# A 64-byte shift for weight units read in 256 columns, and a weight ring taken in strict turn

## The chip, the cores and the metric

The kernel runs on one core of one Trainium2 chip. The metric is the time of one execution in microseconds (us) on the device. Before the change it is 1171.04 us, the median of three runs (1170.99 to 1173.9).

## What is computed

A two-layer transformer block stack over 256 latent tokens and 256 context tokens of width 1024, batch 1, all in fp32. Layer 0 mixes with retention (4 heads, queries and keys of 256, values of 512), layer 1 with neighbourhood attention (32 heads of 32) over a window of the 4 x 64 grid and all context tokens. Each layer ends with an MLP of hidden width 4096 with a squared ReLU. Cut to what matters here:

```python
p = h_lat @ w_in                                # neighbourhood attention, layer 1
q = p[..., :d].reshape(b, rows, GRID_W, nh, hd) * scale
k = p[..., d:2 * d].reshape(b, rows, GRID_W, nh, hd)
v = p[..., 2 * d:].reshape(b, rows, GRID_W, nh, hd)
pc = h_ctx @ (w_in if ctx_out else w_in[:, d:]) # the context gives keys and values too
...
h = jnp.square(jax.nn.relu(x @ w1)) @ w2        # MLP, sketched: 1024 to 4096 to 1024
```

## The kernel before

**Products in three passes.** Every fp32 operand is split into a rounded part `hi` and a remainder `lo`, and `mm3` forms a product as hi·hi + hi·lo + lo·hi, three matmuls into the same PSUM bank. The activations stand transposed in `hTh` and `hTl` (feature by token, 8 chunks of 512 tokens: 256 latent, then 256 context). A product over latent tokens or context tokens alone is 256 columns wide, one over both is 512.

**Weights in units.** `specs` lists the weights in the order in which they are used, as units of 1024 floats per partition (512 KB in all). `fetch(n)` issues the next n: SP's DMA brings the unit into one of four `raw` buffers, ACT copies it to `hi` (a CAST to the matmul's type), and `lows(n)` later lets DVE subtract `hi` from `raw` into `lo`. The tiles come from the pools `hip` and `lop` of WB = 5 buffers each: a new unit gets the buffer that comes free first. The first stage (`class Weights`, layer 0's first head) takes from the same pools. ACT's CAST has to wait until PE has read the buffer's earlier unit for the last time.

**Order.** In the long retention stage a scheduler places instructions; from the end of layer 0's MLP on, `ORDER = (pe, act, dve)` keeps PE, ACT and DVE in the order in which the code is written, so that an instruction that waits holds up all behind it on its engine. SP and POOL have an order of their own.

**Stages by time.** Retention fills the span to about 440 us, layer 0's MLP runs to 792 us, attention to 990 us and layer 1's MLP to the end. The MLP's first half works on 256 hidden features at a time (a pair of 128): `mm1` on latent tokens and on context tokens apart for the first two pairs, on all 512 columns for the others.

**The start of attention.** The units there are, in order: query pair 0 (2 units), first key group pair (2), query pair 1 (2), first values (4), and so on. `q_mm(p, u)` multiplies query pair p by its unit u for the latent tokens, `q_evac(p)` moves the result to `qT` (four ACT instructions for the high part, eight on DVE for the low part). `k_mm(g, a, b)` multiplies the keys of group g by tokens a to b, `k_evac` moves them to `kT`, and `k_part` does both; the context part of the first keys is late. `scores(0)` then multiplies `kT` by `qT` (bank `pqk`) in three passes of four small matmuls: hi·hi, q-hi·k-lo, q-lo·k-hi, and `v_part` multiplies the values (bank `pnv`). The code runs:

```python
    q_mm(1, 0)
    fetch(2)
    lows(1)
    q_mm(1, 1)
    q_evac(1)
    lows(1)
    ...
    for g in range(2):
        fetch(1)
        k_part(g, NLAT, NT)
        lows(1)
```

followed by `scores(0)`, `fetch(1)`, `soften(0)` and `v_part(0, 0)`. The four fetches in this piece are the four units of the first values; the two query units were taken before.

**A shift that is there already.** In layer 1's MLP the first product reads `hTh` from `AT = 7 * LINE` floats into each chunk on (`LINE` is 16 floats, 64 bytes), so that its 256 columns start 448 bytes into a chunk. Elsewhere a 256-column matmul's moving columns and its stationary weights start at the same remainder of 128 bytes.

**Small constants.** `lnT`, `cT`, `scol`, `bcol`, `acol`, `misc`, `lgn` and four `mods` are single tiles in `cpool`, which lies ahead of the big tiles in SBUF.

Of the kernel before, what the change touches and what calls it, by code (L numbers as in the profile page):

```python
# [10 lines left out]
F32 = mybir.dt.float32  # L11
F32R = mybir.dt.float32r
# [5 lines left out]
P = 128  # L18
D = 1024
KC = D // P  # L20
# [4 lines left out]
DK = 256  # L25
DV = 512
# [10 lines left out]
LINE = 16  # L37
# [67 lines left out]
def kernel(  # L105
# [27 lines left out]
    ec = ctx.enter_context  # L133

    WB = 5
    smp = ec(tc.tile_pool(name="smp", bufs=4))
    cpool = ec(tc.tile_pool(name="cpool", bufs=1))
    rawp = ec(tc.tile_pool(name="rawp", bufs=4))
    hip = ec(tc.tile_pool(name="hip", bufs=WB))
    lop = ec(tc.tile_pool(name="lop", bufs=WB))  # L140
    scp = ec(tc.tile_pool(name="scp", bufs=8))
    arena = ec(tc.tile_pool(name="arena", bufs=1))
    dram = ec(tc.tile_pool(name="dram", bufs=1, space=DRAM))
# [8 lines left out]
    def nm(s):  # L152
        uid[0] += 1
        return f"{s}_{uid[0]}"
# [4 lines left out]
    def slot(i, shape, dt, s):  # L159

        return arena.tile(shape, dt, tag=f"s{i}", name=nm(s))

    def scr(s, dt=F32):
        return scp.tile([P, 512], dt, tag="scr", name=nm(s))
# [17 lines left out]

    specs = []

    def w_rows(wt, r0, nr, c0, ncol):
        specs.append((wt[r0 : r0 + nr, c0 : c0 + ncol], nr // P, ncol))

    WI, WO = ret_w_in[0], ret_w_o[0]
    for h in range(RH):
        if h:  # L190
            for u in range(2):
                w_rows(WI, 512 * u, 512, h * DK, DK)
        for u in range(2):
            w_rows(WI, 512 * u, 512, D + h * DK, DK)
        if h:
            for u in range(4):
                w_rows(WI, 256 * u, 256, 2 * D + h * DV, DV)
        for u in range(4):
            w_rows(WI, 256 * u, 256, 4 * D + h * DV, DV)
        for half in range(2):  # L200
            for u in range(2):
                w_rows(WO, h * DV + u * 256, 256, half * 512, 512)

    def spec_w1(l, f0):
        for u in range(2):
            w_rows(mlp_w1[l], 512 * u, 512, f0, 256)

    for hf in range(2):
        for fp in range(8):
            spec_w1(0, hf * 2048 + fp * 256)  # L210
        for half in range(2):
            for u in range(8):
                w_rows(mlp_w2[0], hf * 2048 + u * 256, 256, half * 512, 512)

    NW, NWO = nat_w_in[0], nat_w_o[0]

    def spec_nq(base, gp):
        for u in range(2):
            w_rows(NW, 512 * u, 512, base + gp * 256, 256)

    def spec_nv(half):
        for u in range(4):
# [2 lines left out]
    for kind, i in (  # L225
        ("q", 0), ("k", 0), ("q", 1), ("v", 0), ("k", 1), ("k", 2), ("q", 2), ("v", 1), ("q", 3), ("k", 3)
    ):
        if kind == "v":
            spec_nv(i)
        else:  # L230
            spec_nq(D if kind == "k" else 0, i)
# [4 lines left out]
    for fp in range(16):  # L236
        spec_w1(1, fp * 256)
# [16 lines left out]
    units = []  # L254
# [3 lines left out]
    def fetch(n, in_scratch=False, at=None):  # L258

        for src, k, ncol in specs[len(units) : len(units) + max(n, 0)]:  # L260
            raw = rawp.tile([P, k, ncol], F32, tag="raw", name=nm("raw"))
            sp.dma_start(out=raw[:], in_=src.rearrange("(k p) n -> p k n", p=P))
            if len(units) in scaled_units:
                dve.tensor_mul(
                    out=raw[:], in0=raw[:], in1=scale_row[0].unsqueeze(1).broadcast_to([P, k, ncol])
                )
            if in_scratch or len(units) in scratch_units:
                hi, lo = Rows([scr("hi", F32R) for _ in range(k)]), Rows([scr("lo", F32R) for _ in range(k)])
                for i in range(k):
                    act.copy(out=hi[:, i, :], in_=raw[:, i, :])  # L270
                    pending.append((lo[:, i, :], raw[:, i, :], hi[:, i, :]))
                units.append((hi, lo))
                continue
            if at is None:
                hi = hip.tile([P, k, ncol], F32R, tag="hi", name=nm("hi"))
                lo = lop.tile([P, k, ncol], F32R, tag="lo", name=nm("lo"))
            else:
                both = slot(at, [P, 2, k, ncol], F32R, "hilo")
                hi, lo = both[:, 0], both[:, 1]
            act.copy(out=hi[:], in_=raw[:])  # L280
            pending.append((lo[:], raw[:], hi[:]))
            units.append((hi, lo))
# [32 lines left out]

    ident = cv("ident")

    lnT = cpool.tile([P, 2, 2, 2, KC], F32, tag="lnT", name="lnT")
    cT = cpool.tile([P, KC, 16, 2], F32, tag="cT", name="cT")
    scol = cpool.tile([P, 2, KC], F32, tag="scol", name="scol")  # L320
    bcol = cpool.tile([P, 2, KC], F32, tag="bcol", name="bcol")
    acol = cpool.tile([P, 3, 2, KC], F32, tag="acol", name="acol")
    COLUMNS = (0, 1), (1, 0), (1, 1)
    lns = dram.tile([64, P], F32, tag="lns", name="lns")

# [40 lines left out]
    still = scr("still", F32R)  # L366
    dve.memset(still[:, :256].bitcast(F32), 1.0)

    misc = cpool.tile([P, 40], F32, tag="misc", name="misc")
    mhalf, onecol, lgm = misc[:, 0:1], misc[:, 1:34], misc[:, 36:40]  # L370
    dve.memset(mhalf[:], -0.5)

    lgn = cpool.tile([P, 2, 8], F32, tag="lgn", name="lgn")
    mods = {}
    for l in range(2):
        for w in range(2):
            mods[l, w] = cpool.tile([P, 2, KC, 2], F32, tag=f"mod{l}{w}", name=f"mod{l}{w}")

# [13 lines left out]
    def outside():  # L394
        rows = rpb_in.rearrange("h d c -> h (d c)")
        parts = [slot(i, [P, 4 * NT], F32, "rows") for i in (S_TH, S_TL)]
        neg = parts[0][:, 4 * NT - 2 * P :]
        for r in range(4):
# [121 lines left out]
    def bg_stream():  # L520
# [13 lines left out]
        for step, (l, w, part, offs, n) in enumerate(plan):  # L534
# [7 lines left out]
            if (l, w, part) in EARLY:  # L542
                dve.on = True
                for kk in range(2):
                    for t in range(nt):
                        weigh(spare(t), raw[:, kk, :], t, 2 * (n % 4) + kk, n % 4 == 0 and kk == 0)
                dve.on = False
                if n % 4 == 3:
                    yield
                    for t in range(nt):  # L550
                        folded(red, spare(t), t, 512 * (n // 4), 512)
            else:
                if n == 0:
                    acc = slot(S_VL, [P, 2, D], F32, "acc")
                for t in range(nt):

                    dve.on = n == 0 and (w, part) == (0, 0)
                    weigh(acc[:, t], raw[:].rearrange("p a n -> p (a n)"), t, n, n == 0)
                    dve.on = False
                if n == KC - 1:  # L560
                    for t in range(nt):
                        folded(red, acc[:, t], t, 0, D)
# [118 lines left out]
    def moments(t):  # L681
        mv = smp.tile([P, 2], F32, tag="mv", name=nm("mv"))
        dve.bn_aggr(out=mv[:], in_=stats[t][:])
        return mv, rstd_of(mv, dve)
# [67 lines left out]
    class Weights:  # L752
# [9 lines left out]

        def high(self, cols=slice(0, DK + DV)):
            if cols.start == 0:
                self.hi = hip.tile([P, DK + DV], F32R, tag="hi", name=nm("hi"))
            act.copy(out=self.hi[:, cols], in_=self.raw[:, cols])

        def low(self, cols=slice(0, DK + DV)):
            if cols.start == 0:
                self.lo = lop.tile([P, DK + DV], F32R, tag="lo", name=nm("lo"))  # L770
            dve.tensor_sub(out=self.lo[:, cols], in0=self.raw[:, cols], in1=self.hi[:, cols].bitcast(F32))

    def chunk_loads(k):
# [147 lines left out]
    w = ws[0]  # L921
# [98 lines left out]
    for h in range(RH):  # L1020
# [9 lines left out]
        else:  # L1030
# [15 lines left out]
            for u in range(4):  # L1046
                ((wh, wl),) = take(1)
                for t in range(4):
                    for kk in range(2):
                        k = 2 * u + kk  # L1050
# [137 lines left out]
        else:  # L1188
# [17 lines left out]
            def turn(t):  # L1206
                return [mod_pt(xns[t], half) for half in range(2)]

            def affine(t, pts):
                return [mod_aff(pts[half], half, t, A, B) for half in range(2)]  # L1210
# [19 lines left out]
            f0 = affine(0, p0)  # L1230
# [11 lines left out]
            for half in range(2):  # L1242
                mod_split(f1[half], half, 1, dve)
            take(0, 2)
            fetch(1)
            white(2, shift_of(*m2), m2[1])
            add_to(3, 0, proj(3, 0), pool)
# [5 lines left out]
    def squared(ps, sl):  # L1253
        w = sl.stop - sl.start
        r = scr("r")
        act.activation(out=r[:, :w], in_=ps[:, sl], func=AF.Relu)
        dve.scalar_tensor_tensor(
            out=r[:, :w], in0=ps[:, sl], scalar=0.0, in1=r[:, :w], op0=ALU.max, op1=ALU.mult
        )
        return r[:, :w]  # L1260
# [31 lines left out]
    for hf in range(2):  # L1292
# [9 lines left out]
        if hf == 0:  # L1302
# [18 lines left out]
            r0 = [squared(pb, LAT) for pb in pbs[0]]  # L1321
# [37 lines left out]
        for half in range(2):  # L1359
# [66 lines left out]
            p = turn(0)  # L1426
            mm2(2, 5, held[1])
            f = affine(0, p)
# [7 lines left out]
            p = turn(1)  # L1436
            f = affine(1, p)
# [422 lines left out]
    n = NS - 1  # L1860
# [74 lines left out]
    mv0, r0 = moments(0)  # L1935
# [300 lines left out]
```

## Time and profile before

| | |
|---|---|
| median of three runs | 1171.04 us (1170.99 to 1173.9) |
| the profiled execution | 1175.97 us |
| its span, first to last instruction | 1174.0 us, so 1.97 us lie outside |
| PE busy | 99% of the span, 6687 matmuls |
| DVE, ACT, POOL busy | 72%, 41%, 16% |
| mean granted TensorE clock | 0.995 of full speed |

The span is that of one execution under the profiler. A stretch of PE's time can be shortened only by fewer or quicker matmuls, or by ending a wait of PE. A group's mean duration of one matmul counts it from issue to the end of its drain; how fast they follow one another is read from the chain, where a piece of n matmuls has one duration.

### The profile page before, as it was taken

To read this page: it belongs to the slowest core of one execution; us is meant where nothing else is said; L and a number is where in the kernel's file an instruction comes from. 1 tells how busy PE (TensorE), PEld (TensorE's weight loads), DVE (VectorE), ACT (ScalarE), POOL (GpSimd) and SP (SyncE) were. 2 spreads that over 40 slices of the span, in tenths; PEclk is the share of its full clock that TensorE was granted. 3 is DMA by queue.
4 is the path that set the end of the run, shared out by engine and by line. 5 is a ranking of instruction groups with operands and counts; after the bars stand their busy time and mean duration, and the time that the engine had idled before them with its cause. 6 is when DMAs were issued, how large, how long until landed. Compare 5 with 4: busy or idle time off the path is not lost.

```text
span 1174.0 us, 17497 instructions
## 1 busy us (share of the span) xinstructions
PE 1163.1 (99%) x6687; PEld 983.5 (84%) x6687; DVE 846.2 (72%) x1393; ACT 476.6 (41%) x833; POOL 193.3 (16%) x352
## 2 busy tenths in 40 slices
PE   9999999999999999999999999999999999999997
PEld 6788888888888889888888888889878878999886
DVE  3796687788798878678866775568566578877456
ACT  2653321332223246442112333137466566756341
POOL 0102001010220237600311011121222221000001
PEclk8999999999999999999999999999999999999999
DMA  9943453545355426636666666625234235666761
GB/s 274 261 146 108 144 172 116 147 140 176 112 174 160 133 72 222 223 114 215 182 213 192 203 211 189 210 90 180 72 116 125 84 111 160 212 207 204 241 198 54
DMA packets 134164, 192.54 MB, mean 164 GB/s; under 512 B 7265, under 2 KB 77489, under 8 KB 134081
## 3 DMA queue, kind: packets, MB, share of 16 engines
q1 hardware_dynamic: 129888, 178.36, 48.5%
q0 software_dynamic: 3136, 10.63, 2.9%
q10 hardware_dynamic: 1056, 2.44, 0.7%
q8 instruction: 52, 0.85, 0.3%
q14 instruction: 32, 0.25, 0.1%
HBM read 185.06 MB, written 6.35 MB: 163 GB/s over the span
## 4 chain that ended last, share of the span: by engine, by line
PE 94%; DVE 2%; ACT 1%; DMA 1%; issue 1%; POOL 0%; ACTq 0%; DVEq 0%; SPq 0%
PE p L84 44%; PE pq L84 8%; PE pv L84 8%; PE pw L84 7%; PE pg L84 7%; PE pn L84 5%; PE pnv L84 4%; PE po L84 2%; PE pnw L84 2%; PE ppt L84 1%; PE pS L84 1%; PE pav L84 1%; PE pt L84 1%; PE pada L84 1%; PE pqk L84 1%; PE p1t L84 1%
## 5 line engine op out<-in xcount | busy, mean ns | idle before, releaser
L84 ACT CAST hi<-raw 128x1024 fp32r<-128x1024 f32 (+2 forms) x228 | 231.9, 1033 | 298.8 <-PE p L84 130.8
L84 DVE TENSOR_TENSOR lo<-raw,hi 128x1024 fp32r<-128x1024 f32 (+2 forms) x228 | 272.7, 1212 | 91.2 <-ACT hi L84 91.0
L84 PE MATMUL p<-hi,hid 128*128 128x512 f32 (+1 forms) x780 | 237.9, 386 | 0.0
L84 PEld LDWEIGHTS p<-hi,hid 128*128 128x128 f32 x780 | 145.7, 188 | 29.4
L84 PE MATMUL p<-hTl,hi 128*128 128x256 f32 (+1 forms) x512 | 165.9, 326 | 0.0
L84 PE MATMUL p<-hTh,lo 128*128 128x256 f32 (+1 forms) x512 | 165.9, 326 | 0.0
L84 PE MATMUL p<-hTh,hi 128*128 128x256 f32 (+1 forms) x512 | 162.6, 327 | 0.0
L84 PE MATMUL p<-lo,hid 128*128 128x512 f32 (+1 forms) x390 | 150.5, 386 | 0.0
L84 DVE SCALAR_TENSOR_TENSOR acc<-rawa,scol,acc 128x1024 f32<-128x1024 f32 x56 | 73.4, 1318 | 63.8 <-DMA rawa<-in_ada_w_dram 63.5
L84 PEld LDWEIGHTS p<-hTl,hi 128*128 128x128 f32 x512 | 96.4, 188 | 8.7
L84 PEld LDWEIGHTS p<-hTh,lo 128*128 128x128 f32 x512 | 96.3, 188 | 8.7
L84 PEld LDWEIGHTS p<-hTh,hi 128*128 128x128 f32 x512 | 94.3, 188 | 8.8
L84 PEld LDWEIGHTS p<-lo,hid 128*128 128x128 f32 x390 | 73.3, 188 | 14.7
L84 DVE SCALAR_TENSOR_TENSOR strips<-rawa,scol,strips 128x512 f32<-128x512 f32 x112 | 78.5, 762 | 0.0
L84 ACT CAST hid<-r 128x256 fp32r<-128x256 f32 (+1 forms) x64 | 31.9, 500 | 108.4 <-DVE r L84 108.3
L84 POOL TENSOR_TENSOR rstd<-rstd,misc 128x1 f32<-128x1 f32 x28 | 19.1, 684 | 222.1 <-DVE rstd L84 221.1
L84 PE MATMUL pw<-hi,oh 128*128 128x512 f32 x128 | 50.7, 396 | 0.0
L84 PE MATMUL pg<-hi,hTh 128*128 128x512 f32 x128 | 50.6, 395 | 0.0
L84 PE MATMUL pw<-hi,ol 128*128 128x512 f32 x128 | 50.0, 391 | 0.1
L84 PE MATMUL pg<-hi,hTl 128*128 128x512 f32 x128 | 49.9, 390 | 0.0
L84 PE MATMUL pq<-hTh,hi 128*128 128x512 f32 x128 | 49.7, 399 | 0.1
L84 PE MATMUL pg<-lo,hTh 128*128 128x512 f32 x128 | 49.8, 389 | 0.0
(241 smaller groups left out, 2227.6 us busy)
## 6 DMA issues: line engine op xcount, KB each, us to landing
raw<-in_mlp_w_dram SPq DMA_DIRECT2D x128, 512.0 KB, 4.5
rawa<-in_ada_w_dram SPq DMA_DIRECT2D x80, 512.0 KB, 3.8
raw<-in_ret_w_in_dram SPq DMA_DIRECT2D x42, 512.0 KB, 4.0
raw<-in_nat_w_in_dram SPq DMA_DIRECT2D x24, 512.0 KB, 4.3
rawq<-in_ada_w_dram SPq DMA_DIRECT2D x16, 512.0 KB, 6.0
raw<-in_ret_w_o_dram SPq DMA_DIRECT2D x16, 512.0 KB, 3.5
bias<-rpb_all POOLq DMA_DIRECT2D x16, 256.0 KB, 3.5
raw<-in_nat_w_o_dram SPq DMA_DIRECT2D x8, 512.0 KB, 3.5
```

The costliest lines, as they stand in the source:

```text
L84: r = f(*args, **kwargs)
```

## The change

Three things are changed. The two pools `hip` and `lop` give way to five pools `w0` to `w4` of one buffer each, which holds `hi` and `lo` of one unit side by side with 64 bytes to spare; `wpair` takes them in strict turn, `visits % WB`, whichever is free. The units of the queries, of the first two key groups and of the first MLP's first two pairs are written 64 bytes (`LINE`) further into their place than the others, so that their stationary weights start 64 bytes off the remainder of 128 at which the moving columns start. And the small constants move from `cpool` into pools between the places `w0` to `w3` (448 bytes each), `cT` into a slot of the arena. `cpool` is thereby 2336 bytes shorter, so all big tiles start at addresses that differ by 32 bytes modulo 128 from those of before, all by the same.

```diff
-    hip = ec(tc.tile_pool(name="hip", bufs=WB))
-    lop = ec(tc.tile_pool(name="lop", bufs=WB))
+    wps, gaps = [], []
+    for i in range(WB):
+        wps.append(ec(tc.tile_pool(name=f"w{i}", bufs=1)))
+        if i < 3:
+            gaps.append(ec(tc.tile_pool(name=f"gap{i}", bufs=1)))
...
+    WSLOT = 1024
+    visits = [0]
+
+    def wpair(at=0):
+
+        i = visits[0] % WB
+        visits[0] += 1
+        both = wps[i].tile([P, 2 * WSLOT + (LINE if i < 3 else P)], F32R, tag="w", name=nm("w"))
+        return both[:, at : at + WSLOT], both[:, at + WSLOT : at + 2 * WSLOT]
...
-    def w_rows(wt, r0, nr, c0, ncol):
+    places = {}
+
+    def w_rows(wt, r0, nr, c0, ncol, place=0):
+        places[len(specs)] = place
         specs.append((wt[r0 : r0 + nr, c0 : c0 + ncol], nr // P, ncol))
...
-            spec_w1(0, hf * 2048 + fp * 256)
+            spec_w1(0, hf * 2048 + fp * 256, LINE if hf == 0 and fp < 2 else 0)
...
-            w_rows(NW, 512 * u, 512, base + gp * 256, 256)
+            w_rows(NW, 512 * u, 512, base + gp * 256, 256, LINE if base == 0 or gp == 0 else 0)
...
-                hi = hip.tile([P, k, ncol], F32R, tag="hi", name=nm("hi"))
-                lo = lop.tile([P, k, ncol], F32R, tag="lo", name=nm("lo"))
+                hi, lo = (w.rearrange("p (k n) -> p k n", k=k) for w in wpair(places[len(units)]))
...
-    lnT = cpool.tile([P, 2, 2, 2, KC], F32, tag="lnT", name="lnT")
-    cT = cpool.tile([P, KC, 16, 2], F32, tag="cT", name="cT")
...
+    lnT = gaps[0].tile([P, 2, 2, 2, KC], F32, tag="lnT", name="lnT")
+    cT = arena.tile([P, KC, 16, 2], F32, tag="s1", name="cT")
```

The order of instructions on PE, SP and POOL stays as it was. On ACT, at the start of attention, this stood before (`hi_1060` to `hi_1072` are the four units of the first values, `pn` the banks of queries and keys; "waits" names the semaphores that the instruction itself waits for, PE among them):

```order
L84 CAST hi_1060_6846<-raw_1059_6844 128x1024 [waits DMAHW4_49]
L84 CAST hi_1063_6851<-raw_1062_6849 128x1024 [waits DMAHW5_49,PE_49]
L84 ACTIVATE qT_1027_6615<-pn_1057_6818 128x128 [waits PE_49]
L84 ACTIVATE qT_1027_6615<-pn_1057_6818 128x128
L84 ACTIVATE qT_1027_6615<-pn_1058_6819 128x128 [waits PE_49]
L84 ACTIVATE qT_1027_6615<-pn_1058_6819 128x128
L84 DMA G_1066_6893<-grow10_111 128x1024 [waits DMASW2_49]
L84 CAST hi_1068_6901<-raw_1067_6899 128x1024 [waits DMAHW6_49]
L84 CAST kT_1044_6727<-pn_1070_6904 128x256 [waits PE_49]
L84 CAST hi_1072_6934<-raw_1071_6932 128x1024 [waits DMAHW7_49,PE_49]
L84 CAST kT_1044_6727<-pn_1074_6937 128x256 [waits PE_49]
```

The same place on ACT after the change (`w_924`, `w_926`, `w_930` and `w_933` are the same four units):

```order
L84 CAST w_924_6728<-raw_923_6726 128x1024 [waits DMAHW4_49]
L84 CAST w_926_6732<-raw_925_6730 128x1024 [waits DMAHW5_49,PE_49]
L84 ACTIVATE qT_895_6501<-pn_921_6700 128x128 x2
L84 ACTIVATE qT_895_6501<-pn_922_6701 128x128 x2
L84 DMA G_928_6773<-grow10_129 128x1024 [waits DMASW2_49]
L84 CAST w_930_6781<-raw_929_6779 128x1024 [waits DMAHW6_49,PE_49]
L84 CAST kT_910_6611<-pn_931_6783 128x256
L84 CAST w_933_6813<-raw_932_6811 128x1024 [waits DMAHW7_49]
L84 CAST kT_910_6611<-pn_934_6815 128x256
```

The rows stand in the same order, but `qT` and `kT` no longer wait for PE themselves, and the third unit's CAST now does: the CASTs `w_926` and `w_930` wait for PE instructions that stand later in PE's order than those that `qT` and `kT` need. By the turn, `w_926` goes into the place of the first unit of the first keys and `w_930` into that of the second; before, `hi_1063` and `hi_1068` took the buffers of the two units of query pair 1.

On DVE, in retention's second head, this stood before (`t12` and `qkl` belong to the rotation of queries and keys, `lo_224` is a weight unit):

```order
L84 TENSOR_TENSOR qkl_205_1320<-t12_217_1389,qkh_204_1319 128x256 [waits Activation_49]
L84 TENSOR_TENSOR lo_224_1418<-raw_222_1415,hi_223_1417 128x1024 [waits DMAHW3_49,PE_49,Activation_49]
L84 TENSOR_TENSOR t12_218_1398<-pq_207_1322,cst1_82 128x256 [waits Activation_49]
L84 TENSOR_TENSOR t12_218_1398<-pq_207_1322,cst1_82 64x256 x2
L84 TENSOR_TENSOR qkl_205_1320<-pq_207_1322,qkh_204_1319 128x256
L84 TENSOR_TENSOR t12_218_1398<-t12_218_1398 128x256 [waits DVE_49]
```

After the change, the same place on DVE (`w_199` is the same unit):

```order
L84 TENSOR_TENSOR qkl_184_1317<-t12_193_1383,qkh_183_1316 128x256 [waits Activation_49]
L84 TENSOR_TENSOR t12_194_1392<-pq_186_1319,cst1_100 128x256 [waits Activation_49]
L84 TENSOR_TENSOR t12_194_1392<-pq_186_1319,cst1_100 64x256 x2
L84 TENSOR_TENSOR qkl_184_1317<-pq_186_1319,qkh_183_1316 128x256
L84 TENSOR_TENSOR t12_194_1392<-t12_194_1392 128x256 [waits DVE_49]
L84 TENSOR_TENSOR w_199_1411<-raw_198_1409,w_199_1411 128x1024 [waits DMAHW3_49,Activation_49]
```

The unit's subtraction stands five instructions later. The same happens to some units of the other heads, and in layer 0's MLP some units' CAST and subtraction change places with the neighbouring step of a squared ReLU.

## Rows read from the trace of the kernel before

**Rows 1.** The page: span, busy time by engine, shares of the last chain.

```profile
span 1174.0 us, 17497 instructions
...
PE 1163.1 (99%) x6687; PEld 983.5 (84%) x6687; DVE 846.2 (72%) x1393; ACT 476.6 (41%) x833; POOL 193.3 (16%) x352
...
PE 94%; DVE 2%; ACT 1%; DMA 1%; issue 1%; POOL 0%; ACTq 0%; DVEq 0%; SPq 0%
```

**Rows 2.** PE's groups by shape: count, busy us, mean ns, idle ahead.

```profile
L84 PE MATMUL p<-hi,hid 128*128 128x512 f32 x756 | 233.6, 389 | 0.0
...
L84 PE MATMUL p<-hTh,hi 128*128 128x256 f32 x288 | 75.4, 279 | 0.0
...
L84 PE MATMUL pn<-hTh,hi 128*128 128x256 f32 x96 | 27.5, 287 | 0.0
...
L84 PE MATMUL pnw<-hilo,oTl 128*128 128x512 f32 x2 | 0.8, 392 | 0.0
```

**Rows 3.** Chain in order of time, first MLP's first pairs: start, us, what.

```profile
443.34 5.75 PE p L84 x48
```

**Rows 4.** Chain, layer 1's MLP, where the columns start 448 bytes on.

```profile
1002.81 5.66 PE p L84 x48
...
1008.90 61.10 PE p L84 x539
```

**Rows 5.** PE's timeline at the first MLP's start: start us, us, what.

```profile
446.29 0.28 PE L84 MATMUL p<-hTh,lo 128*128 128x256 f32 x1
```

**Rows 6.** DVE's timeline at the same place.

```profile
444.85 1.23 DVE L84 TENSOR_TENSOR lo<-raw,hi 128x1024 fp32r<-128x1024 f32 x1
```

**Rows 7.** PE's timeline at query pair 1.

```profile
805.84 0.28 PE L84 MATMUL pn<-hTl,hi 128*128 128x256 f32 x1
806.13 0.38 PE L84 MATMUL pn<-hTh,lo 128*128 128x256 f32 x1
```

**Rows 8.** DVE's timeline from there to the first scores.

```profile
804.86 2.35 DVE L84 TENSOR_TENSOR lo<-raw,hi 128x1024 fp32r<-128x1024 f32 x2
...
812.21 1.14 DVE L84 SCALAR_TENSOR_TENSOR qT<-pn,qT 128x64 fp32r<-128x64 f32 x8
...
815.22 0.43 DVE L84 TENSOR_TENSOR kT<-pn,kT 128x256 fp32r<-128x256 f32 x1 [0.75 <-ACT kT L84]
```

**Rows 9.** Chain at the same place, to the first scores.

```profile
806.13 11.53 PE pn L84 x94
817.66 0.77 PE pqk L84 x7
```

**Rows 10.** PE's timeline at the first scores.

```profile
815.94 0.28 PE L84 MATMUL pn<-hTh,lo 128*128 128x256 f32 x1
...
817.59 0.84 PE L84 MATMUL pqk<-kT,qT 32*128 32x416 f32 x12
```

**Rows 11.** ACT's timeline there; in brackets idle time and what ended it.

```profile
809.83 2.00 ACT L84 CAST hi<-raw 128x1024 fp32r<-128x1024 f32 x2
811.73 0.45 ACT L84 ACTIVATE qT<-pn 128x128 fp32r<-128x128 f32 x2
...
812.37 1.08 ACT L84 CAST hi<-raw 128x1024 fp32r<-128x1024 f32 x1
...
816.14 1.05 ACT L84 CAST hi<-raw 128x1024 fp32r<-128x1024 f32 x1 [0.95 <-PE pn L84]
817.69 0.37 ACT L84 CAST kT<-pn 128x256 fp32r<-128x256 f32 x1 [0.51 <-PE pn L84]
```

**Rows 12.** DVE's timeline in retention's second head, the subtraction of the unit shown.

```profile
145.36 1.23 DVE L84 TENSOR_TENSOR lo<-raw,hi 128x1024 fp32r<-128x1024 f32 x1 [0.52 <-ACT hi L84]
```

**Rows 13.** PE's timeline where that unit's low part is first read.

```profile
165.97 0.39 PE L84 MATMUL pv<-lo,hTh 128*128 128x512 f32 x1
```

**Rows 14.** Windows near the start: busy (count) of PE, PEld, DVE, ACT, POOL; PEclk.

```profile
6.00:9.00 3.00, 2.06 (x21) 1.48 (x21) 0.55 (x4) 0.00 (x0) 0.00 (x0) 0.76 1.17 306
...
15.00:18.00 3.00, 3.00 (x22) 1.94 (x24) 0.00 (x0) 0.83 (x1) 0.00 (x0) 0.53 1.21 292
```

More of the change, by code (lines that the diff above doesn't have):

```diff
@@ L202, with spec_w1 @@
                 w_rows(WO, h * DV + u * 256, 256, half * 512, 512)
-    def spec_w1(l, f0):
+    def spec_w1(l, f0, place=0):
         for u in range(2):
-            w_rows(mlp_w1[l], 512 * u, 512, f0, 256)
+            w_rows(mlp_w1[l], 512 * u, 512, f0, 256, place)
     for hf in range(2):
         for fp in range(8):
-            spec_w1(0, hf * 2048 + fp * 256)
+            spec_w1(0, hf * 2048 + fp * 256, LINE if hf == 0 and fp < 2 else 0)
         for half in range(2):
@@ L316 @@
     ident = cv("ident")
-    lnT = cpool.tile([P, 2, 2, 2, KC], F32, tag="lnT", name="lnT")
-    cT = cpool.tile([P, KC, 16, 2], F32, tag="cT", name="cT")
-    scol = cpool.tile([P, 2, KC], F32, tag="scol", name="scol")
-    bcol = cpool.tile([P, 2, KC], F32, tag="bcol", name="bcol")
-    acol = cpool.tile([P, 3, 2, KC], F32, tag="acol", name="acol")
+    lnT = gaps[0].tile([P, 2, 2, 2, KC], F32, tag="lnT", name="lnT")
+    cT = arena.tile([P, KC, 16, 2], F32, tag="s1", name="cT")
+    scol = gaps[1].tile([P, 2, KC], F32, tag="scol", name="scol")
+    bcol = gaps[2].tile([P, 2, KC], F32, tag="bcol", name="bcol")
+    acol = gaps[0].tile([P, 3, 2, KC], F32, tag="acol", name="acol")
     COLUMNS = (0, 1), (1, 0), (1, 1)
@@ L367 @@
     dve.memset(still[:, :256].bitcast(F32), 1.0)
-    misc = cpool.tile([P, 40], F32, tag="misc", name="misc")
+    misc = gaps[2].tile([P, 3 * LINE], F32, tag="misc", name="misc")
     mhalf, onecol, lgm = misc[:, 0:1], misc[:, 1:34], misc[:, 36:40]
     dve.memset(mhalf[:], -0.5)
-    lgn = cpool.tile([P, 2, 8], F32, tag="lgn", name="lgn")
+    lgn = gaps[2].tile([P, 2, 8], F32, tag="lgn", name="lgn")
     mods = {}
@@ L376 @@
         for w in range(2):
-            mods[l, w] = cpool.tile([P, 2, KC, 2], F32, tag=f"mod{l}{w}", name=f"mod{l}{w}")
+            mods[l, w] = gaps[1 + l * w].tile([P, 2, KC, 2], F32, tag=f"mod{l}{w}", name=f"mod{l}{w}")
     RR = [cpool.tile([P, 2, D], F32, tag=f"R{t}", name=f"R{t}") for t in range(2)]
@@ L764, in high @@
             if cols.start == 0:
-                self.hi = hip.tile([P, DK + DV], F32R, tag="hi", name=nm("hi"))
+                self.hi, self.lo = (w[:, : DK + DV] for w in wpair())
             act.copy(out=self.hi[:, cols], in_=self.raw[:, cols])
         def low(self, cols=slice(0, DK + DV)):
-            if cols.start == 0:
-                self.lo = lop.tile([P, DK + DV], F32R, tag="lo", name=nm("lo"))
             dve.tensor_sub(out=self.lo[:, cols], in0=self.raw[:, cols], in1=self.hi[:, cols].bitcast(F32))
```

## The prediction, made before the kernel ran

> **What bounds the kernel now.** I read the page first: PE is busy for 99% of a span of 1174.0 us and holds 94% of the chain that ended last [rows 1]. The reader is to see that ACT at 41% and DVE at 72% matter only where PE stands and waits for one of their instructions; everything else is a matter of how fast matmuls follow one another. So I took the groups by shape next, to see which matmuls the change touches, then the chain in time, because a group's mean (279 ns for 256 columns [rows 2]) includes the drain and overlaps the next matmul, whereas a piece of the chain divided by its count gives the pitch. Last I read the timelines of PE, ACT and DVE in the few microseconds around each place where a shifted unit or a ring place changes hands.
>
> The pitch of 256-column matmuls is not one number. In the first MLP's first pairs 48 take 5.75 us [rows 3], 119.8 ns each. For query pair 1 and the first keys 94 records take 11.53 us [rows 9]; the code has 96 there, two of which left no record, so 120.1 ns. In layer 1's MLP, where the moving columns already start 64 bytes off the remainder of 128 of the weights, 539 take 61.10 us, 113.4 ns; but a stretch of 48 just ahead of it, with the same offset, takes 5.66 us, 117.9 ns [rows 4].
>
> **The change part by part.**
>
> *The shift.* It touches 480 matmuls: 192 in the first MLP (two pairs, 48 on latent and 48 on context tokens each), 192 in the four query pairs, 96 in the first keys, the last 96 as 32 for each of the three passes; the group of 96 for bank pn [rows 2] is one pass of these 288. What an offset gives is bounded by the rows above: 119.8 or 120.1 less 113.4 is 6.5 ns at best, less 117.9 it is 2.0 ns, and below that nothing at all, since the two pitches at one offset show that something else sets a part of it. The 117.9 stretch is short and stands between transposes, as do the 24 and 48 of the first MLP's first pieces; the 113.4 one is long. I take 2.0 ns for the first 72 matmuls of the MLP and 6.5 ns for the other 120, which run on behind.
>
> What of it reaches the end:
> - First MLP: PE first reads one unit's low part at 446.29 [rows 5], and DVE ends it at 444.85 + 1.23 = 446.08 [rows 6], 0.2 us ahead. Some 48 matmuls stand before that read, and 48 x 2.0 = 0.1 us fits into it. So 72 x 2.0 + 120 x 6.5 = 0.9 us (all at 6.5: 1.25, less the 0.1 by which 48 x 6.5 overruns the slack; all at 2.0: 0.4).
> - Query pair 0 and the latent part of the first keys, 96 matmuls: nothing. At 805.84 PE issues a matmul and the next only at 806.13 [rows 7], 0.17 us later than the pitch, for the first of the two subtractions that DVE starts at 804.86 and ends, both, at 807.21 [rows 8], so the first near 806.05. That chain of DVE is not paced by PE. What is saved before it is waited away.
> - Query pair 1 and the context part of the first keys, 96 matmuls from 806.13: the 82 up to the last read at 815.94 [rows 10] move what follows. 82 x 2.0 = 0.16 or 82 x 6.5 = 0.53; I take 0.35.
> - Two more query pairs, 48 matmuls each among transposes: 96 x 2.0 = 0.2 us (at 6.5: 0.6).
>
> Together 1.45 us; bounds 0 and 2.3.
>
> *The ring in strict turn.* This is the term on the other side, and the order on ACT shows it. Before, the second unit of the first values got the buffer of a query unit, and its CAST is the second of the pair that starts at 809.83 and takes 2.00 [rows 11]. Now its place is that of the first unit of the first keys, which PE reads for both groups' context part, last at 815.94 for 0.28 us [rows 10], so to 816.22. ACT runs in program order there: behind the waiting CAST stand the four `qT` of `q_evac(1)`, the CAST of the third unit and the `kT` of group 0, and behind these on DVE eight `qT` subtractions, the unit's low part and `kT`'s low part. PE waits for them in `scores(0)`, which began at 817.59 [rows 10], directly behind the keys (the chain has 817.66 [rows 9]).
>
> From the release at 816.22: the CAST holds ACT for 0.95 (its 1.05 [rows 11], less the 0.1 by which neighbours overlap): 817.17. Four `qT` and the DMA issue: from 811.73 to 812.37 it was 0.64 [rows 11]; 817.81. The third unit's CAST 0.95, its place, free at about 817.66, no longer decides: 818.76. `kT` 0.37 [rows 11]: 819.13. So the first pass of the scores is 1.5 us late. The second pass needs `kT`'s low part. DVE: eight `qT` subtractions, 1.14 [rows 8], begin behind the first `qT` at about 817.6 and end at 818.7; the second unit's low part takes 1.2 (two take 2.35 [rows 8]), to 819.85; `kT`'s low part 0.43 [rows 8], to 820.28. Without the wait this pass would start a third of the 12 matmuls' time (0.84 [rows 10]) behind 817.59, at 817.87. The stall is 820.28 - 817.87 = **2.4 us**. If DVE does the unit's low part while ACT is at the third CAST, as assumed, nothing hides the rest; if ACT's and DVE's steps overlap better than one after the other, the first pass's 1.5 us is the lower bound; an upper one is 3.2, with the third unit's subtraction (1.2) ahead of the fourth's reading and partly on PE's path. What is late next: the third and fourth value units' low parts, done at about 821.5 and 823.1 (1.2 each, with another `kT` of 0.43 between them). `v_part` follows the scores, from about 820.8, and reads them behind 12 and 18 of its 512-column matmuls; these have twice the columns of those that take 113 ns [rows 4], so at least 0.22 each, which is 823.4 and 824.8: not late.
>
> Elsewhere the turn costs nothing that I can find. In retention and the MLPs a unit is read once, in the order in which it came, so the place whose turn it is is also the one free longest; only the first keys outlive the units behind them.
>
> *Moved rows.* In retention some subtractions stand five DVE instructions later. The unit shown was done at 145.36 + 1.23 = 146.59 [rows 12] and first read at 165.97 [rows 13]: five instructions, each no longer than that 1.23, hide in 19 us. Without that cover PE would wait up to 6 us a head. The swaps in the MLP are by one step, and I cost them at nothing on the same ground.
>
> *The constants and the 32 bytes.* No instruction is added; small operands move to other addresses. All big tiles start elsewhere by 32 bytes modulo 128, but stand to one another as before. No row shows what an absolute start costs. I take nothing; the price for being wrong is large, because 3,942 matmuls have 512 columns (from 756 in the largest of the 34 groups to 2 in the smallest [rows 2]): 1 ns on each is 3.9 us either way.
>
> **The sum.** 2.4 - 1.45 = +0.95 us: against the profiled execution's 1175.97 (its span of 1174.0 [rows 1] and the 1.97 around it) 1176.9. That execution stands 4.9 us above the median of the runs, so the same step from 1171.04 gives **1172.0 us**. A measurement of this kernel can tell about 0.3%, 3.5 us, from no change, and this is well inside.
>
> One rule speaks against any gain. The pitch at the one offset is 113.4 to 117.9 and without it 119.8 to 120.1 [rows 3, 4, 9], which reads as if the moving columns and the weight load got in each other's way. The Trainium skill, "SBUF — State Buffer", section "Who interferes with whom", gives PE two independent read ports, one for the moving operand and one for the weight load, and says that PE never waits on anyone. By that the offset is without effect, and the sum would be the ring's term alone, +2.4. The rows don't agree so far as two stretches of one shape differ by 6.5 ns; that the offset is the cause they don't show.
>
> **The rivals.**
> - *The shift gives nothing, the stall stays*: the 113.4 of layer 1 comes from the long undisturbed run and not from the offset. For it: 117.9 at the same offset [rows 4]. Against: the level differs from 119.8 even there. +2.4: 1173.5. Chance 0.14.
> - *Full shift, no stall*: 6.5 ns everywhere, and ACT's late CAST is covered. For it: only that it is 2.4 us on three engines in series, which I put together by hand. Against: the order of ACT, in which nothing can pass the CAST. -2.3: 1168.7. Chance 0.10.
> - *The new start of the big tiles speeds the 512-column matmuls*: 1 ns off 3,942 is -3.9, with the sum above 1168.1; 2 ns give 1164.1. No row shows such a level. Chance 0.09. The same with the other sign, 1175.9: chance 0.05.
> - *Slower, by the clock*: near the start PE was busy for 2.06 of 3 us in the stretch from 6 to 9, in which the granted clock fell to 0.76, and it was still 0.53 at 15 to 18 [rows 14]; 0.5 is the lower of the two levels, 1.2 of 2.4 GHz. If a stall of 2.4 us at 817 brings the same, some 10 us (from the second half of the one stretch to near the end of the other) at half speed cost 5 us: +6, 1177.0. It decides as soon as PE's idle time there reaches the 0.94 us of that stretch and the chip treats it alike. Against: at the start PE has only begun, here it is full on both sides of the stall. Chance 0.08.
>
> **Chances and range.** My forecast has 0.54: 1170.9 to 1173.4, from 0.2 us below no change (stall 2.2 and gain 2.3) to the stall with little gain. The range to hold 8 in 10 takes in both first rivals and the milder half of a layout effect: 1168.3 to 1175.6. Faster by over 0.3%, below 1167.5: part of the layout rival and the tail of the second, 0.09. Slower, above 1174.6: clock, layout and a larger stall, 0.15. Within: 0.76.
>
> **What would show it.** In the chain after the change: a wait of 1.5 to 2.5 us before and inside `pqk` near 817, released by ACT's or DVE's `kT`; on ACT a CAST held by PE at about 810 to 816, and the four `qT` behind it at 817 instead of 811.7. Pitches of 113 to 118 ns for p at 440 to 460 and for pn; still 120 there means that the shift is without effect. The prediction is wrong if the windows behind 817 show a clock below 1, or if a 512-column pitch moves.

## The result: 1174.76 us, 0.25% slower

The median of 22 runs is 1174.76 us (1172.79 to 1178.76), that of before 1171.69 (1170.94 to 1175.88, 22 runs): +3.1 us, ratio 1.0025 (95% interval 1.0019 to 1.0032). The forecast was 1172.0, from 1171.04; so the side was right and the step is three times the forecast one. The time lies in the wide range (1168.3 to 1175.6, meant to hold 8 in 10), but above the narrow one (1170.9 to 1173.4) that belonged to the forecast itself. The granted clock is not the same in each execution: in 5 of the 22 runs its mean is 0.999 and the time 1172.79 to 1173.83, in the other 17 it is 0.998 or less and the time 1174.35 or more.

The page of the changed kernel's profiled execution (1176.35 us) hardly differs from [rows 1]:

```profile
span 1174.3 us, 17495 instructions
...
PE 1161.9 (99%) x6687; PEld 981.5 (84%) x6687; DVE 845.9 (72%) x1393; ACT 478.1 (41%) x833; POOL 191.4 (16%) x352
```

The two spans are alike by chance, which the windows near the start show (columns as in [rows 14], the granted clock being the number behind the busy times of the five engines):

```profile
6.00:9.00 3.00, 2.83 (x42) 1.75 (x40) 0.86 (x5) 0.00 (x0) 0.00 (x0) 1.00 1.15 304
...
15.00:18.00 3.00, 3.00 (x16) 2.31 (x15) 2.12 (x5) 1.96 (x3) 0.00 (x0) 1.00 1.19 295
```

The clock there is 1.00, where before it was 0.76 and 0.53. That belongs to the one profiled execution of before and not to its kernel: in 69 other runs of before, timed beside the experiments, the mean clock is 0.998 or 0.999, and not 0.995. It puts the changed kernel's execution ahead: it comes to query pair 1 at 801.40, before was there at 806.13 [rows 9]. So what follows compares stretches and not spans. PE's waits in the changed kernel (whom it waited for, us in total, times, longest) name the place:

```profile
PE pqk L84 <- ACT kT L84: 1.7, 1, 1.7
...
PE pqk L84 <- DVE kT L84: 0.6, 1, 0.6
```

ACT's timeline there shows the CAST that stands until PE has read the first keys, and the row of work behind it (the counterpart of [rows 11]):

```profile
805.11 1.06 ACT L84 CAST w<-raw 128x1024 fp32r<-128x1024 f32 x1
811.01 1.05 ACT L84 CAST w<-raw 128x1024 fp32r<-128x1024 f32 x1 [4.85 <-PE pn L84]
...
811.97 0.77 ACT L84 ACTIVATE qT<-pn 128x128 fp32r<-128x128 f32 x4
812.61 1.06 ACT L84 CAST w<-raw 128x1024 fp32r<-128x1024 f32 x1
813.54 0.40 ACT L84 CAST kT<-pn 128x256 fp32r<-128x256 f32 x1
```

DVE's timeline, the three steps behind it (the counterpart of [rows 8]):

```profile
812.44 1.14 DVE L84 SCALAR_TENSOR_TENSOR qT<-pn,qT 128x64 fp32r<-128x64 f32 x8 [5.01 <-ACT qT L84]
813.50 1.22 DVE L84 TENSOR_TENSOR w<-raw,w 128x1024 fp32r<-128x1024 f32 x1
814.63 0.42 DVE L84 TENSOR_TENSOR kT<-pn,kT 128x256 fp32r<-128x256 f32 x1
```

PE's timeline, end of the keys and the scores (the counterpart of [rows 10]):

```profile
812.06 0.28 PE L84 MATMUL pn<-hTh,w 128*128 128x256 f32 x1
814.00 0.46 PE L84 MATMUL pqk<-kT,qT 32*128 32x416 f32 x4 [1.66 <-ACT kT L84]
815.10 1.07 PE L84 MATMUL pqk<-kT,qT 32*128 32x416 f32 x8 [0.64 <-DVE kT L84]
```

This is the stall of the forecast, step by step: from the release at 811.01 the `kT` of ACT starts 2.53 us later (forecast 818.76 - 816.22 = 2.54), the second pass 4.09 us later (forecast 4.06). But the 24 value matmuls behind it are slow too, as the chain shows:

```profile
801.40 9.59 PE pn L84 x82
...
815.10 1.07 PE pqk L84 x8
816.17 8.23 PE pnv L84 x24
824.40 0.77 PE pqk L84 x11
825.17 5.67 PE pnv L84 x24
```

24 matmuls in 8.23 us, and the next 24 of the same kind in 5.67. The windows say why (granted clock as above, behind the five busy times):

```profile
812.00:815.00 3.00, 0.80 (x7) 0.33 (x6) 2.56 (x11) 3.00 (x9) 0.00 (x0) 0.97 0.46 173
815.00:818.00 3.00, 2.90 (x13) 2.02 (x14) 3.00 (x5) 2.40 (x3) 0.00 (x0) 0.50 0.58 181
818.00:821.00 3.00, 3.00 (x9) 2.32 (x8) 3.00 (x10) 2.62 (x8) 1.02 (x2) 0.50 0.78 252
821.00:824.00 3.00, 3.00 (x13) 2.48 (x12) 2.23 (x2) 0.00 (x0) 2.48 (x5) 0.90 0.94 287
```

PE was busy for 0.80 of 3 us, and the clock then stood at 0.50, the lower of its two levels, for some 6 us. This is the rival "Slower, by the clock" of the prediction. Here it goes together with the stall; whether it follows from it, and what each is worth, the experiments had to say.

### The profile page after: what moved, and what is told of

The parts are those of the page before. It is cut to its first block, busy times and chain, and to the rows that moved or that the text cites. A ratio compares the mean times of both kernels' runs of the same rounds, so it can differ in the third digit from the quotient of the medians.

```text
span 1174.3 us, 17495 instructions
## 1 busy us (share of the span) xinstructions
PE 1161.9 (99%) x6687; PEld 981.5 (84%) x6687; DVE 845.9 (72%) x1393; ACT 478.1 (41%) x833; POOL 191.4 (16%) x352
## 4 chain that ended last, share of the span: by engine, by line
PE 92%; DVE 3%; ACT 2%; DMA 1%; issue 1%; POOL 0%; DVEq 0%; ACTq 0%; SPq 0%
PE p L84 43%; PE pq L84 8%; PE pv L84 8%; PE pw L84 7%; PE pg L84 7%; PE pnv L84 4%; PE pn L84 4%; PE po L84 2%; PE pnw L84 2%; PE ppt L84 1%; PE pS L84 1%; PE pav L84 1%; PE pada L84 1%; PE pqk L84 1%; PE pt L84 1%; PE p1t L84 1%
## 5 line engine op out<-in xcount | busy, mean ns | idle before, releaser
L84 ACT CAST w<-raw 128x1024 fp32r<-128x1024 f32 (+2 forms) x224 | 231.7, 1040 | 323.3 <-PE p L84 159.1
L84 DVE TENSOR_TENSOR w<-raw,w 128x1024 fp32r<-128x1024 f32 (+2 forms) x224 | 271.7, 1220 | 96.8 <-ACT w L84 96.5
L84 PE MATMUL p<-w,hid 128*128 128x512 f32 (+1 forms) x1158 | 260.0, 386 | 0.0
L84 PEld LDWEIGHTS p<-w,hid 128*128 128x128 f32 x1158 | 214.8, 188 | 43.6
L84 PE MATMUL p<-hTh,w 128*128 128x256 f32 (+1 forms) x1024 | 238.2, 327 | 0.0
L84 PEld LDWEIGHTS p<-hTh,w 128*128 128x128 f32 x1024 | 171.6, 188 | 17.5
L84 PE MATMUL p<-hTl,w 128*128 128x256 f32 (+1 forms) x512 | 165.7, 326 | 0.0
L84 PEld LDWEIGHTS p<-hTl,w 128*128 128x128 f32 x512 | 96.2, 188 | 8.7
L84 PE MATMUL pq<-hTh,w 128*128 128x512 f32 x256 | 80.1, 392 | 0.4 <-DVE hTh L84 0.4
L84 PE MATMUL pw<-w,oh 128*128 128x512 f32 x256 | 79.9, 393 | 0.0
```

Source lines behind the costliest of these rows:

```text
L84: r = f(*args, **kwargs)
```

## The experiments

**Theory 1:** the strict turn makes ACT wait for the first keys' place; PE's idle time lowers the clock behind it; the two cost some 5 us, and the shift gives back some 2. **Theory 2:** the new places of constants and big tiles cost the time. **Theory 3:** the shift brings the wait, as it makes PE early. "Before" is the kernel before, timed on the same chip beside each group of runs.

**The turn by hand.** One line more in `wpair`, for the units from the first values on (number 128 of `specs`):

```diff
         i = visits[0] % WB
+        if len(units) >= 128:
+            i = (1, 4, 0, 2, 3)[(visits[0] - 1) % WB]
         visits[0] += 1
```

> The change with one thing altered: from the first value unit of attention on, the turn of the ring is w1, w4, w0, w2, w3, so that no value unit waits for a place of the first keys. Theory 1 (the ring's wait and the clock that falls behind it cost some 5 us, the shift gives back some 2): the wait of 1.7 and 0.6 us at the first scores is gone, the granted clock is 1.00 from 812 to 824, the pitch of pn stays at 113 to 117 ns, and the time is 1.5 to 2.5 us below before (ratio 0.998). Theory 2 (the new places of constants and big tiles cost the time, the wait is swallowed elsewhere): still 1 us or more above before.

Measured: 1170.67 us, before 1171.71: 1.04 less, ratio 0.9994 (0.9982 to 1.0006). The waits for `kT` are gone from PE's list, and the chain has

```profile
801.71 10.94 PE pn L84 x94
812.65 0.77 PE pqk L84 x9
813.42 5.67 PE pnv L84 x24
819.09 0.77 PE pqk L84 x11
```

so 96 matmuls (94 records) in 10.94 us, 114.0 ns each with the restart (113.3 on the timeline behind it), and 11.71 us from 801.71 to the values, where the change took 14.77. The place of the value units is the cause; theory 2 falls. The gain is half of what was expected. Once more, for its interval:

> The run with the turn by hand once more, for its interval. First time 1.0 us below before by the medians, ratio 0.9994 (0.9982 to 1.0006). Theory 1: again 0.5 to 1.5 us below. If the first result was chance: not below before.

Measured: 1170.64, before 1171.35: 0.71 less, ratio 0.9992 (0.9982 to 1.0003). Twice the median is below before, but each interval just includes 1: a gain is likely, and not shown.

**No shift.** Every unit starts its place, the strict turn stays:

```diff
-                hi, lo = (w.rearrange("p (k n) -> p k n", k=k) for w in wpair(places[len(units)]))
+                hi, lo = (w.rearrange("p (k n) -> p k n", k=k) for w in wpair())
```

> The change without the shift: every unit starts its place, the strict turn stays. Theory 1: the wait at the first scores and the lower clock behind it stay, the pitch of pn and of the first MLP's pairs is back at 120 ns: 1.5 to 2.5 us slower than the change, about 5 us (ratio 1.004) above before. Theory 3 (the shift itself brings the wait, since quicker keys make ACT late): no lower clock at 815 to 821, time within 1 us of before.

Measured: 1176.04, before 1171.71: +4.33, ratio 1.0032 (1.0019 to 1.0045). The chain, slow values included:

```profile
802.26 11.55 PE pn L84 x94
...
817.56 8.11 PE pnv L84 x24
```

The wait (1.6 and 0.6 us in PE's list) and the fall of the clock (0.50 from 816 to 822 in the windows) are there without the shift: theory 3 falls. The 96 matmuls are back at 120 ns. The shift is worth 1.3 us here, a little less than theory 1 had it.

**Turn by hand and no shift**, both edits together:

> Turn by hand and no shift: what is left of the change are the new places of the constants and of the big tiles, and hi and lo in one tile. Theory 1: equal to before within 0.5 us, pitch of pn 120 ns. Theory 2 (layout costs): 2 us or more above before.

Measured: 1171.96, before 1171.71: +0.25, ratio 1.0005 (0.9993 to 1.0017): the new layout costs nothing that can be measured. The chain has

```profile
801.45 11.54 PE pn L84 x94
```

**The wait filled.** PE still waits for `kT`, but does idle matmuls meanwhile, into a bank that is overwritten later:

```diff
         for i, (a, b) in enumerate(((0, 0), (0, 1), (1, 0))):
+            for _ in range((14, 5, 0)[i] if n == 0 else 0):
+                pe.matmul(av[0][:, :256], lhsT=hTh[:, 0, :P], rhs=hTh[:, 0, :256], start=True, stop=True)
```

> The change, with 14 extra matmuls of 256 columns ahead of the first pass of the first scores and 5 ahead of its second pass (into the bank of pav, whose content is not used yet): some 1.6 and 0.6 us of PE work where PE stood idle for 1.7 and 0.6 us. The passes still wait for kT. Theory 1a (the fall of the granted clock behind the wait is caused by PE's idle time, and costs its own 2 us or so beside the wait): the clock stays 1.00 from 815 to 824, the 24 matmuls behind the scores take 5.7 us as before the change and not 8.2, and the time is 1 to 2.5 us below the change (1172.3 to 1173.8). Theory 1b (something else lowers the clock there, or it does not count): the clock falls as in the change, time equal to the change or above it.

Measured: 1173.74, before 1171.53: +2.21, ratio 1.0020 (1.0009 to 1.0031). The chain:

```profile
801.34 10.94 PE pn L84 x94
812.29 1.67 PE pav L84 x14
813.96 0.52 PE pqk L84 x3
814.48 0.79 PE pav L84 x5
815.27 0.58 PE pqk L84 x7
815.85 5.68 PE pnv L84 x24
```

And the window that had 0.50 in the change:

```profile
815.00:818.00 3.00, 3.00 (x21) 2.19 (x20) 3.00 (x4) 2.35 (x3) 0.00 (x0) 1.00 0.58 178
```

The scores start where they did, 12.62 us behind the start of the keys' piece (change: 814.00 - 801.40 = 12.60), so the wait for ACT is untouched; the clock stays at 1.00 and the values take 5.68. The mean clock of all the runs says the same: it is 0.997 or less in 11 of the 22 runs of the change and in 7 of the 12 without the shift, but in only 1 of the 12 with the wait filled, and in none of the 36 with the turn by hand (with and without the shift) nor of the 69 of before. Theory 1a holds: where PE works instead of standing idle, the clock seldom falls. The time alone would not show it: the change was 3.07 us above its before, this run 2.21, and the two intervals overlap.

From the start of the piece to the values it takes 14.51, against 11.71 without the wait, so 2.80 us more. Not all of that is the wait, since the filling ends late. DVE's timeline and PE's have

```profile
814.58 0.42 DVE L84 TENSOR_TENSOR kT<-pn,kT 128x256 fp32r<-128x256 f32 x1
```

```profile
815.20 0.65 PE L84 MATMUL pqk<-kT,qT 32*128 32x416 f32 x8
```

so `kT` is whole at 815.00, and the second pass starts 0.20 behind that, held up by the idle matmuls; in the change it starts 0.05 behind. Counted from the start of the piece it is 13.86 here (815.20 - 801.34) and 13.70 there (815.10 - 801.40). Without these 0.16 us the wait alone is 2.64 us in the profiled executions.

**The fetch behind the evacuation.** Strict turn, but the second value unit's fetch is written behind `q_evac(1)`, so that `qT` doesn't stand behind its CAST:

```diff
     q_mm(1, 0)
-    fetch(2)
+    fetch(1)
     lows(1)
     q_mm(1, 1)
     q_evac(1)
+    fetch(1)
     lows(1)
```

> The change, with the fetch of the second value unit written behind the evacuation of query pair 1, in strict turn as before. The CAST still waits for the first keys' last read, but the four qT and DVE's eight subtractions no longer stand behind it. Theory 1: ACT's chain is shorter by 0.64 us and DVE's by 1.1: a first wait of about 1.0 us and hardly a second one, so 1 us or more below the change if the clock falls, 3 us or so if it does not (1171.5 to 1173.7). If the clock falls at any idle time it stays at 0.50 for some 6 us here as well; if it goes by how long PE stands, it may stay 1.00. Rival (the wait is for the place and not for what stands behind it on ACT and DVE): no difference to the change.

Measured: 1173.04, before 1171.53: +1.51, ratio 1.0012 (1.0003 to 1.0021). PE's timeline and the window behind it:

```profile
817.49 1.11 PE L84 MATMUL pqk<-kT,qT 32*128 32x416 f32 x12 [1.41 <-ACT kT L84]
```

```profile
818.00:821.00 3.00, 3.00 (x19) 2.32 (x20) 3.00 (x6) 2.89 (x4) 0.00 (x0) 1.00 0.80 202
```

One wait of 1.41 us, none for DVE's `kT`, and the clock stays at 1.00 in this execution (1177.11 us, the slowest of the twelve; in 2 of the twelve the mean clock is 0.997 or less). ACT's timeline says what is left of the wait:

```profile
814.76 1.05 ACT L84 CAST w<-raw 128x1024 fp32r<-128x1024 f32 x1 [3.63 <-PE pn L84]
...
816.12 1.04 ACT L84 CAST w<-raw 128x1024 fp32r<-128x1024 f32 x1 [0.31 <-PE pn L84]
817.07 0.37 ACT L84 CAST kT<-pn 128x256 fp32r<-128x256 f32 x1
```

The second value unit's CAST is over in time; it is the third one's, which waits 0.31 us more for PE's last read of the second key unit, that `kT` now stands behind. The expected 1.0 us took 0.64 off the old wait and left out that this CAST has a release of its own to wait for. The execution has a second wait of 0.90 us, at 833.10: PE for ACT's `natv`, ACT for DVE, and DVE for a transfer of `bias`. No other profiled execution has it, so whether it comes from the edit or from this execution stays open.

**Two offsets.** The turn by hand; shifted units on places w3 and w4 at 128 bytes, on w0 to w2 at 64:

```diff
+        if i >= 3:
+            at = 2 * at
         both = wps[i].tile([P, 2 * WSLOT + (LINE if i < 3 else P)], F32R, tag="w", name=nm("w"))
```

> As the run with the turn by hand, but the shifted units that fall on places w3 and w4 stand 128 bytes on, those on w0 to w2 64 bytes. First MLP: pair 1 has both units at 64, pair 2 both at 128. If the remainder of 128 bytes sets the pitch: pair 1 at 113 to 118 ns, pair 2 at 120. If any offset will do: both at 113 to 118. If the offset is without effect and the run is what counts: both alike too, as pair 2 without a shift would show in the run without shift.

One execution, 1174.53 us, whose time is not compared. Here the piece ahead of the scores is the cleanest place: its first 24 matmuls are at 128 bytes, the next 24 at 64. PE's timeline, rows of `hTl`, one in three matmuls:

```profile
805.42 0.27 PE L84 MATMUL pn<-hTl,w 128*128 128x256 f32 x1
...
807.55 0.28 PE L84 MATMUL pn<-hTl,w 128*128 128x256 f32 x1
...
808.24 0.28 PE L84 MATMUL pn<-hTl,w 128*128 128x256 f32 x1
...
810.28 0.28 PE L84 MATMUL pn<-hTl,w 128*128 128x256 f32 x1
```

18 matmuls between the rows of each pair: 118.3 ns at 128 bytes, 113.3 at 64. So 64 is better than 128, but 128 is not the 120.0 of no offset: neither clean case. The first MLP, for which the expectation was written, agrees: on the timeline the pair at 128 has 118 to 119 ns, the pair at 64 has 117.8 on latent tokens and 113.3 to 113.5 on context tokens.

**Five offsets.** As above, with 64, 32, 32, 192 and 256 bytes on w0 to w4:

```diff
+        at = at // LINE * (64, 32, 32, 192, 256)[i] // 4
         both = wps[i].tile([P, 2 * WSLOT + (LINE if i < 3 else P)], F32R, tag="w", name=nm("w"))
```

> The turn by hand, and the shifted units at other offsets by their place: w0 64 bytes, w1 and w2 32, w3 192, w4 256. In the undisturbed piece of 96 matmuls of pn ahead of the first scores the order of units is then 256 (24 matmuls), 64 (24), and 32 and 192 by turns (12 each). If the remainder of 128 bytes sets the pitch: 256 at 120 ns, 192 at 113.3 as 64, 32 unknown. The run with two offsets gave 117.5 at 128 and 113.3 at 64, so the remainder of 128 alone is in doubt: if the distance counts, 192 and 256 come out at 117.5 or less too.

One execution, 1172.31 us. The piece's 96 matmuls (94 records):

```profile
802.57 11.37 PE pn L84 x94
```

that is 118.4 ns on average. The unit at 64 bytes, which had 113.3 before, has 117.8 here (18 matmuls from 805.76 to 807.88 on the timeline); it stands behind one at 256. The 48 matmuls at 32 and 192 bytes by turns have 117.9 (42 from 808.59 to 813.54), so 192 is not as quick as 64 was: that expectation failed.

**One unit at 256.** All at 64 bytes but for w4:

```diff
+        if i == 4:
+            at = 4 * at
         both = wps[i].tile([P, 2 * WSLOT + (LINE if i < 3 else P)], F32R, tag="w", name=nm("w"))
```

> The turn by hand with all shifted units at 64 bytes, but for those on place w4, which stand 256 bytes on. In the piece of 96 matmuls of pn ahead of the first scores the first 24 are then at 256 and the other 72 at 64. In the run with five offsets the unit at 64 in this piece had 118 ns behind one at 256, in the run with two offsets 113.3 behind one at 128. If the level is carried on from the matmuls before (it is set where the stream starts, and holds): 118 in all 96. If each unit's offset sets its own pitch: 118 in the first 24 and 113.3 in the other 72, and the 118 of the unit at 64 in the run with five offsets is left unexplained.

One execution, 1170.70 us. PE's timeline of the piece, at the ends of the first 24 and of the other 72:

```profile
801.31 0.28 PE L84 MATMUL pn<-hTl,w 128*128 128x256 f32 x1
...
803.47 0.28 PE L84 MATMUL pn<-hTl,w 128*128 128x256 f32 x1
...
804.18 0.28 PE L84 MATMUL pn<-hTl,w 128*128 128x256 f32 x1
...
811.95 0.28 PE L84 MATMUL pn<-hTl,w 128*128 128x256 f32 x1
```

18 matmuls in 2.16 us are 120.0 ns at 256 bytes; 66 in 7.77 are 117.7 at 64, where the run with the turn by hand had 113.3 at the same addresses. So the offset doesn't set the pitch alone, and the level is held over 72 matmuls. That what ran before sets it too is likely, and not shown: in this piece all five profiled executions with 64 bytes throughout have 113.3, and both with 256 ahead 117.7 or 117.8. But the level is not simply carried on, since 120.0 became 117.7, and behind the unit at 128 bytes the pitch fell to 113.3. And it can differ between two executions of one kernel: the chains of the turn by hand and of its repetition have, for the same 48 matmuls of the first MLP,

```profile
439.34 5.60 PE p L84 x48
```

```profile
438.91 5.69 PE p L84 x48
```

116.7 and 118.5 ns on average; half of the 48 run at 113.9 in the first and at 117.9 in the second. With one execution of each kernel this rival, chance, is not excluded.

## Why the prediction came out as it did

The account, from medians, each against the before timed beside it: the wait +3.25 (wait filled less turn by hand, 2.21 + 1.04), the lower clock +0.86 (change less wait filled, 3.07 - 2.21), the shift -1.29 (turn by hand with and without it) and the layout +0.25. That these add up to 3.07 is no test: by the way they are formed, they must. There is one test: the strict turn has the same price with the shift, 4.11 (3.07 + 1.04), and without, 4.08 (4.33 - 0.25). These are differences of medians; by the intervals above each is uncertain by 1 to 2 us, so the price of the strict turn is shown by the times, the agreement to 0.03 is better than it had to be, and the single 0.86 and -1.29 rest on what the traces show of the clock and of the pitch.

- **The ring in strict turn** was the right mechanism at the right place, and ACT's and DVE's steps came as summed, to 0.03 us. Its size was right too: the second pass starts 13.70 us behind the start of the piece, and 11.20 with the turn by hand (10.94 and a third of 0.77), so it is 2.5 us late for the forecast 2.4. The values were late by 2.64 with the clock at 1.00; by the medians it is 3.25, of which some 0.16 is the filling's own.
- **The step that failed is the sum**, which left out the clock. It stood among the rivals as a case of its own with a chance of 0.08 and 5 us, in addition to the stall. It came true, with less: 3.0 us in the profiled execution (the 24 value matmuls 8.23 instead of 5.67, the last two passes of the scores 1.00 instead of 0.58 on the timelines), but 0.86 in the median (some 1.0 with the filling's 0.16 counted back), since not every execution shows the same fall: the runs' mean clock goes from 0.995 to 0.999 (one stands at 0.973, with a time like the others'). I had the row of what idle time does near the start [rows 14] and still took the stall's price to be the stall. The remark that "here it is full on both sides of the stall" was no protection. The prediction had named a clock below 1 behind 817 as a sign that it is wrong, and by that sign it was. That the time still lies in the wide range is in part luck: with the profiled execution's fall in every run, the step would be about 4.3 us (2.64 + 2.98 - 1.29, an estimate) and the time 1176.0, outside it.
- **The shift**: forecast 1.45, measured 1.29. The way to it was partly right: nothing from what lies before 806 [rows 7, 8], and between 2.0 and 6.5 ns in the rest. The split by stretches was a guess, and two errors in it cancelled: the first MLP's pairs ran at 117.7 on the timelines of the changed kernel and of the turn by hand, but for 24 matmuls of the latter (I had given 120 of them 6.5 ns), query pair 1 and the keys at 113.3 (I had taken two thirds of the most that it could be), and the two other query pairs at 113.3 to 113.7 (I had taken 2.0 ns). By these pitches the MLP gives 0.4 us for the forecast 0.9 and the rest 1.2 for the forecast 0.55, so that the total came near is luck.
- **The first rival**, no effect of the offset, is refuted: two kernels that differ in the offset alone, the turn by hand with and without the shift, have 113.3 and 120.0 ns in the same 96 matmuls. There the measurement differs from the Trainium skill, "SBUF — State Buffer", section "Who interferes with whom", by whose rule of independent ports they would be equal, and it decides.
- **The layout rivals**: +0.25 within an interval of 0.9993 to 1.0017, which holds neither -3.9 nor +3.9 us; the 24 value matmuls of 512 columns take 5.67 us in the new layout with full clock, and in the old one too:

```profile
818.42 5.67 PE pnv L84 x24
```

- **Full shift, no stall** is what the turn by hand does, with 1.0 and 0.7 us for the forecast 2.3.
- **The moved rows** in retention and the MLP cost nothing that the waits show.

What stays open is why the same operands run at 113.3 in one execution and at 117.7 in another, and why the clock falls behind the same wait in some executions only.

## What to carry to other kernels

A ring taken in turn is safe only where units die in the order in which they were born. One that is read late (here keys that wait for the context) must not lie ahead of a unit that an in-order engine converts early, as all that stands behind that conversion waits with it. And where PE is the bound, a wait's price can be its length and what the clock takes behind it: look at the granted clock of the windows that follow it, and try filling the wait to tell the two apart.

## What was not expected of the hardware

- PE idle for 1.66 and 0.64 us, close together, was followed by some 6 us at the clock's lower level; one wait of 1.41 us was not, in the execution profiled; filled with matmuls, the longer wait was not either. Over all runs the fall comes and goes: the mean clock is 0.997 or less in 11 of 22 runs with the longer wait and in 1 of 12 with it filled.
- 256-column matmuls of one shape start every 113.3, 117.7 or 120.0 ns. With weights and columns at the same remainder of 128 bytes, as in attention and the first MLP before the change, 120.0; at an offset of 64 bytes 113.3 or 117.7, at the same addresses, and in one piece the lower pitch was lost when the unit ahead stood at 256; at 128 bytes 118.3, at 32 and 192 by turns 117.9, at 256 bytes 120.0 and, in another run, about 118.9 (18 matmuls in 2.14 us). The last four are from one execution each.
